# First projection of a decoder layer: two token parts in one 512-column matmul, and the bias rows copied from DRAM to DRAM

## The chip, the core and the metric

One core of a Trainium2 chip runs the whole layer in one launch. The metric is the device time of one execution in microseconds (us); lower is better. Engines are called as in the profile: PE (TensorE matmuls), PEld (its weight loads), DVE (VectorE), ACT (ScalarE), POOL (GpSimd, here an issuer of DMAs) and SP (SyncE, the issuer of the weight loads).

## The reference, cut to what matters

The layer takes x of 512 tokens by 2048 features, all in float32:

```
proj = x @ w_in                       # 2048 -> 12288 columns
u, gate_b, gate_c, q, k, v = split(proj)
y_conv = gate_b * causal_conv3(gate_c * u)
o_g    = dilated window attention of 3 groups x 8 heads, with a relative-position bias
x1 = layernorm(alpha * x + concat(y_conv, y_attn) @ w_out)
x2 = layernorm(alpha * x1 + conv_ffn(x1))      # w_up: 2048 -> 11264, w_down: 5632 -> 2048
```

The change touches `x @ w_in` and the table of bias rows (8 heads by 383 or 255 values for each of three groups) that the attention reads along its diagonals.

## The kernel before, in words

**The product.** Each float32 operand is split into a high part (rounded to the type that PE reads at full rate) and a low part (the remainder). A product a*b is taken as a_hi*b_hi + a_lo*b_hi + a_hi*b_lo. Weights go through `Op.front` (ACT writes `whi`, line 191) and `Op.back` (DVE writes `wlo`, line 194); for some operands DVE first forms a difference of two raw blocks (`tt`, line 181). The tokens are split once, at the start, into tiles X[name] = (high, low), each [128, 8, 256].

**Seven products in place of eight.** The first projection (w_in) and the up projection (w_up) are walked in pairs of 128-column blocks: 48 pairs for w_in, 44 for w_up. A pair is a 2x2 block product (two halves of the features, two halves of the tokens) done with seven products in the order `MAIN = [1, 5, 6, 3, 7, 4, 2]`. `product` (line 317) runs one: for each of 8 chunks of 128 features, three matmuls of 256 columns (lines 326 to 328): `whi` on the high tokens, `whi` on the low tokens, `wlo` on the high tokens, all summed into one half of a PSUM bank. A pair uses two banks, m (regions x1, x2) and n (x3, x4). After products 1, 5, 6 and 7 ACT copies the region to SBUF (`snap`, line 374). When a bank is complete, `combine` adds bank and copy on DVE: `bands` (line 572, one add of 512 columns per bank) for most pairs, `bands1` (line 581, two strided adds of 256 per bank) for the 24 of the 36 q, k and v pairs whose tokens are regrouped by stride 4.

**Order.** The program order of each engine is written by hand. `free` calls `pump`, which issues the next weight loads (three raw tiles of 1 MB, SP), and the `tt`, `whi` and `wlo` of operands up to four products ahead of PE; `later(n, fn)` and `tick` put a piece of work n products later, so a `combine` is issued behind the next product. Pair 0 is done plainly, pairs 1 to 5 have products 1 and 2 done early (before the other token tiles are ready), pairs 6 to 47 run all seven.

**Bias rows.** After the last of 12 convolution pairs `bias_setup` runs three times, some two pairs apart. It loads two small tables into one output tile (`otile1`, three slots shared with the pairs' outputs), a small matmul (line 560) and a DVE add (line 561) give 8 rows, and line 563, on POOL's queue, copies them to DRAM so that each of the 8 rows stands there 128 times (`seq_d[g]`: 8 heads x 128 copies x 384). The attention reads `seq_d` much later (lines 634 to 637). Pair outputs leave on the same POOL queue (`qkv_d`, line 611).

Of the kernel before, what the change touches and what calls it, by code (L numbers as in the profile page):

```python
# [12 lines left out]
F32 = mybir.dt.float32  # L13
# [67 lines left out]

class Chunks:
    def __init__(self, tiles, j):
        self.tiles, self.j = tiles, j

    def __getitem__(self, at):
        k = at[1]
        if isinstance(k, slice):  # L90
            return self.tiles[k.start // 2][:, self.j]
        return self.tiles[k // 2][:, self.j, k % 2]


@with_exitstack
def layer_kernel(ctx: ExitStack, tc: tile.TileContext, xT, x, w_in, w_out, w_up, w_down, cw, fw, lnp, lnc, table,
# [209 lines left out]

    pairb = {}

    def region(p, name):
        rg = pairb.setdefault(p, {})  # L310
        b = "m" if name in ("x1", "x2") else "n"
        if b not in rg:
            rg[b + "i"], rg[b] = get_bank()
        return rg[b][:, 256:] if name in ("x1", "x3") else rg[b][:, :256]


    def product(p, q, X, last):
        op = take()
        for q in q if isinstance(q, str) else [q]:
            xn, _, reg = PROD[q]  # L320
            xh, xl = X[xn]
            first = not _banks(q) & set(pairb.get(p, {}))
            ps = region(p, reg)
            for k in range(8):
                w = slice(k * P, (k + 1) * P)
                mm(ps, op.hi[:, w], xh[:, k], start=first and k == 0, stop=False, skip_group_check=True)  # L326
                mm(ps, op.hi[:, w], xl[:, k], start=False, stop=False, skip_group_check=True)  # L327
                mm(ps, op.lo[:, w], xh[:, k], start=False, stop=last and k == 7, skip_group_check=True)  # L328
        return op
# [33 lines left out]
                tick()  # L363
                hook()

    def run_pairs(pl, X, stile, otile, bands, done, hook=None):
        for p, seq, pre in pl:
            if pre or _plain(seq):
                continue
            sn = {b: stile(b).rearrange("p (a t) -> p a t", a=2) for b in "mn"}  # L370

            def snap(q):
                b, i = SNAP[q]
                nc.scalar.activation(sn[b][:, i], region(p, PROD[q][2]), AF.Copy)  # L374

            if 1 not in seq:
                snap(1)
            box = {"todo": 2}

            def combine(p, b, sn, box):  # L380
                if "o" not in box:
# [58 lines left out]
    def s_alloc(X, pools):  # L440
        for n in ("S2", "S4"):
            tiles = [None] * 4
            X[n] = (Chunks(tiles, 0), Chunks(tiles, 1))
        X["pools"] = pools

    def s_first(X, raw, k):
# [25 lines left out]
        low(X, "S4", ks, s4)  # L472

    def xtile(pool, n):
        return tuple(pool.tile([P, 8, 256], F32R, tag=n + s, name=nm(n + s)) for s in "hl")

# [53 lines left out]
        plan_work(XR[i], s_rest, X, raw, 2 * i)  # L530
    hook = schedule(todo)

    def keep1():
        return tp.tile([P, 2, 256], F32, tag="kp", name=nm("kp"), bufs=PRE1[0])
# [7 lines left out]
    def stile1(b):  # L542
        return tp.tile([P, 512], F32, tag="s" + b, name=nm("s" + b), bufs=2)

    def otile1():
        return tp.tile([P, 4, 256], F32, tag="o", name=nm("o"), bufs=3)
# [1 line left out]
    def bias_setup(g=0):  # L548
        if g == 0:
            held["tb"] = tp.tile([32, 3 * NH], F32, name="tb")  # L550
            nc.gpsimd.dma_start(held["tb"], table)
        a, b = [0, LA, LA + LB, LTOT][g:g + 2]
        v = otile1().rearrange("p a b -> p (a b)")
        oh, mk = v[:32, 0:b - a], v[:NH, 512:512 + b - a]
        nc.sync.dma_start(oh, onehot[:, a:b])
        nc.sync.dma_start(mk, mask[:, a:b])

        def finish():
            i, ps = get_bank()
# [54 lines left out]
    run_pairs(plan1, X, stile1, otile1, bands1, done1)  # L614
    ph1.close()


# [214 lines left out]

    a1s, chs, zas, zbs, exs = (ExitStack() for _ in range(5))
    a1p = mkpool(a1s, "a1p")
    A1h = a1p.tile([P, 2, 8, 256], F32R, tag="h", name="A1h")
    A1l = a1p.tile([P, 2, 8, 256], F32R, tag="l", name="A1l")
    chp = mkpool(chs, "chp")
    zbp = mkpool(zbs, "zbp")
    zap = mkpool(zas, "zap")
# [121 lines left out]
    s_alloc(X, {"S2": yap, "S4": xrp})  # L961
    s3p = mkpool(zas, "s3p")
    X["S3"] = xtile(s3p, "S3")
    X["A11"], X["A12"] = (A1h[:, 0], A1l[:, 0]), (A1h[:, 1], A1l[:, 1])

    todo = {}
    for i in range(4):
# [21 lines left out]
    def act_first(p, q):  # L989
        if p < FT - 1:  # L990
            return
        if q == 2:
            act_load(0, xrp, "S1h", nc.gpsimd)
            act_load(1, xrp, "S1l", nc.gpsimd)
            for s in "hl":
                act[s] = a1p.tile([P, 2, 4, S], F32R, tag=s, name=nm("A" + s))
        if q in (6, 3):
            n = (6, 3).index(q)
            act_split(n, act["h"][:, n], act["l"][:, n])
# [200 lines left out]
```

## Time and profile before

| | us |
|---|---|
| three runs | 2672.46, 2673.99, 2676.10 (median 2673.99) |
| profiled execution | 2674.91 |
| its span, first to last instruction | 2673.0 |
| PE busy | 2624.3 (98%) |
| DVE busy | 2015.5 (75%) |
| ACT busy | 1159.3 (43%) |

A sum of expected savings is made against the profiled execution, 2674.91 us, since the durations come from it. Busy is the time in which at least one instruction of the engine ran; the stages have different limits, so these shares are averages. The first projection takes about the first 1020 us, attention and the output projection follow up to about 1260, the up projection up to about 2120, and the down projection the rest.

### The profile page before, as it was taken

How to read it: one execution, taken by the hardware profiler on the slowest of the kernel's cores; microseconds unless marked ns; L12 is line 12 of the kernel's file. 1: busy time of each engine (PE TensorE's matmuls, PEld its weight loads, DVE VectorE, ACT ScalarE, POOL GpSimd, SP SyncE). 2: the span in 40 equal slices, each digit the busy share in tenths (PEclk: the TensorE clock that was granted, in tenths of full speed). 3: DMA queues.
4: the chain of work that ended last, by engine and by line, in shares of the span. 5: the costliest groups of instructions: out<-in, count | busy, mean ns of one | idle time of the engine just before them, and what ended most of it. 6: DMA issues, size and time to landing. Idle time of an engine off the chain costs nothing.

```text
span 2673.0 us, 45078 instructions
## 1 busy us (share of the span) xinstructions
PE 2624.3 (98%) x19114; PEld 2497.2 (93%) x19114; DVE 2015.5 (75%) x2293; ACT 1159.3 (43%) x1617; POOL 124.4 (5%) x214
## 2 busy tenths in 40 slices
PE   9999889999999999999999999999999999999998
PEld 8999789999999998888999999999999998888886
DVE  7987557777777777666899888888888875675557
ACT  5444334444444444434655555555555553222220
POOL 0000000000000002221000000000000000000000
PEclk9999989999999999999999999999999999999999
DMA  7433653333333338644543333333333354434331
GB/s 240 166 103 128 111 138 125 134 129 132 135 123 139 134 119 312 221 160 160 182 144 131 117 123 111 123 123 108 126 119 111 127 181 156 149 142 148 120 126 63
DMA packets 70905, 376.69 MB, mean 141 GB/s; under 512 B 10608, under 2 KB 14440, under 8 KB 36016
## 3 DMA queue, kind: packets, MB, share of 16 engines
q1 hardware_dynamic: 51680, 311.47, 34.0%
q0 software_dynamic: 19024, 62.34, 7.3%
q8 instruction: 150, 2.46, 0.4%
q14 instruction: 51, 0.42, 0.1%
HBM read 324.95 MB, written 48.81 MB: 140 GB/s over the span
## 4 chain that ended last, share of the span: by engine, by line
PE 88%; DVE 5%; DMA 4%; ACT 1%; issue 1%; SPq 0%; DVEq 0%; POOL 0%; ACTq 0%
PE bk L326 21%; PE bk L328 21%; PE bk L327 21%; PE bk L423 8%; PE bk L421 8%; PE bk L422 8%; DMA raw<-in_w_in_dram 2%; DMA seq_d<-o 2%; DVE wlo L194 1%; DVE tt L181 1%; PE bk L744 1%; PE bk L690 1%; PE bk L674 0%; ACT whi L191 0%; PE bk L736 0%
## 5 line engine op out<-in xcount | busy, mean ns | idle before, releaser
L191 ACT ACTIVATE whi<-raw 128x1024 fp32r<-128x1024 f32 x394 | 416.0, 1058 | 631.9 <-PE bk L423 219.0
L194 DVE TENSOR_TENSOR wlo<-raw,whi 128x1024 fp32r<-128x1024 f32 x394 | 480.7, 1223 | 216.0 <-ACT whi L191 215.9
L194 DVE TENSOR_TENSOR wlo<-tt,whi 128x1024 fp32r<-128x1024 f32 x360 | 440.5, 1224 | 210.1 <-ACT whi L191 209.5
L191 ACT ACTIVATE whi<-tt 128x1024 fp32r<-128x1024 f32 x360 | 379.6, 1054 | 220.1 <-PE bk L327 122.7
L326 PE MATMUL bk<-S,whi 128*128 128x256 f32 x1440 | 409.2, 284 | 12.4 <-ACT sm L374 11.5
L327 PE MATMUL bk<-S,whi 128*128 128x256 f32 x1440 | 408.4, 284 | 0.0
L328 PE MATMUL bk<-S,wlo 128*128 128x256 f32 x1440 | 408.4, 284 | 0.0
L326 PEld LDWEIGHTS bk<-S,whi 128*128 128x128 f32 x1440 | 277.5, 193 | 13.6 <-ACT sm L374 11.9
L327 PEld LDWEIGHTS bk<-S,whi 128*128 128x128 f32 x1440 | 277.5, 193 | 0.0
L328 PEld LDWEIGHTS bk<-S,wlo 128*128 128x128 f32 x1440 | 277.4, 193 | 0.0
L181 DVE TENSOR_TENSOR tt<-raw,tt 128x1024 f32<-128x1024 f32 x180 | 219.1, 1217 | 36.6 <-DMA raw<-in_w_in_dram 36.6
L326 PE MATMUL bk<-A22h,whi 128*128 128x256 f32 x752 | 212.8, 283 | 0.0
L327 PE MATMUL bk<-A22l,whi 128*128 128x256 f32 x752 | 212.8, 283 | 0.0
L328 PE MATMUL bk<-S3h,wlo 128*128 128x256 f32 x752 | 212.8, 283 | 0.0
L327 PE MATMUL bk<-S3l,whi 128*128 128x256 f32 x752 | 212.8, 283 | 0.0
L326 PE MATMUL bk<-S3h,whi 128*128 128x256 f32 x752 | 212.8, 283 | 0.0
L328 PE MATMUL bk<-A22h,wlo 128*128 128x256 f32 x752 | 212.8, 283 | 0.0
L328 PE MATMUL bk<-S1h,wlo 128*128 128x256 f32 x720 | 205.1, 285 | 6.2 <-DVE wlo L194 6.2
L326 PE MATMUL bk<-A1h,whi 128*128 128x256 f32 x720 | 205.2, 285 | 0.6 <-ACT S L932 0.6
L326 PE MATMUL bk<-S1h,whi 128*128 128x256 f32 x720 | 204.7, 284 | 0.0
L327 PE MATMUL bk<-S1l,whi 128*128 128x256 f32 x720 | 204.7, 284 | 0.0
L328 PE MATMUL bk<-A1h,wlo 128*128 128x256 f32 x720 | 204.4, 284 | 0.0
(225 smaller groups left out, 6435.4 us busy)
## 6 DMA issues: line engine op xcount, KB each, us to landing
raw<-in_w_in_dram SPq DMA_DIRECT2D x97, 1024.0 KB, 4.9
raw<-in_w_up_dram SPq DMA_DIRECT2D x89, 1024.0 KB, 5.3
raw<-in_w_down_dram SPq DMA_DIRECT2D x44, 1024.0 KB, 4.9
qkv_d<-o POOLq DMA_DIRECT2D x36, 512.0 KB, 4.3
raw<-in_w_out_dram SPq DMA_DIRECT2D x16, 1024.0 KB, 6.8
act_d<-z POOLq DMA_DIRECT2D x44, 256.0 KB, 5.2
qk<-qkv_d SPq DMA_DIRECT2D x7, 1536.0 KB, 10.3
ar<-act_d SPq DMA_DIRECT2D x9, 1024.0 KB, 7.0
```

The lines of the kernel that those rows point to most:

```text
L181: nc.vector.tensor_sub(self.src, v[0], prev)
L191: nc.scalar.activation(self.hi, self.src, AF.Copy)
L194: nc.vector.tensor_sub(self.lo, self.src, self.hi.bitcast(F32))
L326: mm(ps, op.hi[:, w], xh[:, k], start=first and k == 0, stop=False, skip_group_check=True)
L327: mm(ps, op.hi[:, w], xl[:, k], start=False, stop=False, skip_group_check=True)
L328: mm(ps, op.lo[:, w], xh[:, k], start=False, stop=last and k == 7, skip_group_check=True)
L421: mm(banks[n], yh[:, tt], op.hi[:, w], start=first and i == 0, stop=False)
L422: mm(banks[n], yh[:, tt], op.lo[:, w], start=False, stop=False)
L423: mm(banks[n], yl[:, tt], op.hi[:, w], start=False, stop=last and i == 1)
L690: mm(ps[:, o:o + P], qk[:, 2 + 2 * g, rs], qk[:, 3 + 2 * g, rs], start=True, stop=True)
L744: nc.tensor.transpose(ps[:, i * P:(i + 1) * P], src[:, n, s:s + P], ident)
```

## The change

In pairs 6 to 47 of the first projection the high and the low tokens lie in one tile, and one 512-column matmul streams both; its halves go to the two halves of a bank, and the third matmul (256 columns) adds to the second half. Each region takes a bank of its own, so a pair uses four. ACT copies whole banks after products 1, 5 and 6, and a copy of x1 just ahead of one of the sums; for each of four output blocks DVE adds a bank and a copy (512 columns), and then the two halves (256 columns each). Pairs 0 to 5 and the up projection keep three matmuls a chunk. The bias rows go to a small DRAM table first, and from there to their 128 copies by a DRAM-to-DRAM copy whose outer dimension is the 128 copies. Two tiles of the up projection are merged into one each; nothing else of it changes.

```diff
+    def product_wide(p, q, X, last):
+        op = take()
+        xn, _, reg = PROD[q]
+        first = reg not in pairb.get(p, {})
+        ps = wide_region(p, reg)
+        for k in range(8):
+            w = slice(k * P, (k + 1) * P)
+            mm(ps.rearrange("p (a t) -> p a t", a=2), op.hi[:, w], X[xn].both(k), start=first and k == 0, stop=False,
+               skip_group_check=True)
+            mm(ps[:, 256:], op.lo[:, w], X[xn][0][:, k], start=False, stop=last and k == 7, skip_group_check=True)
+        return op
...
+    WSUM = {(0, 0): ("x2", 1), (1, 1): ("x1", 5), (0, 1): ("x4", "x1"), (1, 0): ("x3", 6)}
+    def run_wide(p, seq, X, stile, otile, put_block, done, hook):
...
+        def combine(block):
...
+            reg, other = WSUM[block]
+            if other == "x1":
+                u = stile("u")
+                nc.scalar.activation(u, pairb[p][other], AF.Copy)
+            else:
+                u = sn[other]
+            nc.vector.tensor_add(u, pairb[p][reg], u)
+            put_block(p, box["o"], block, u)
...
+            op = product_wide(p, q, X, PROD[q][2] not in {PROD[j][2] for j in left})
+            if q in (1, 5, 6):
+                sn[q] = stile(str(q))
+                nc.scalar.activation(sn[q], pairb[p][PROD[q][2]], AF.Copy)
+            for block, need in WNEED.items():
+                if block not in sent and not need & left:
+                    sent.add(block)
+                    later(2, functools.partial(combine, block))
...
     def xtile(pool, n):
-        return tuple(pool.tile([P, 8, 256], F32R, tag=n + s, name=nm(n + s)) for s in "hl")
+        return Wide(pool.tile([P, 2, 8, 256], F32R, tag=n, name=nm(n)))
...
-            nc.gpsimd.dma_start(seq_d[g, :, :, :b - a], mk[:, None].to_broadcast([NH, P, b - a]))
+            nc.gpsimd.dma_start(seq1_d[g, :, :b - a], mk)
+            nc.gpsimd.dma_start(seq_d[g, :, :, :b - a].rearrange("h p n -> p h n"),
+                                seq1_d[g, None, :, :b - a].to_broadcast([P, NH, b - a]))
...
+    def block1(p, o, block, u):
+        f, h = block
+        if PAIRS[p][2] == 0:
+            nc.vector.tensor_add(o[:, 2 * f + h], u[:, :256], u[:, 256:])
+            return
+        ov = o.rearrange("p a t -> p (a t)").rearrange("p (f r m) -> p f r m", f=2, r=4)
+        ua, ub = (u[:, 256 * i:256 * i + 256].rearrange("p (m r) -> p r m", r=4) for i in range(2))
+        nc.vector.tensor_add(ov[:, f, :, 64 * h:64 * h + 64], ua, ub)
```

## Rows read from the trace of the kernel before

**Rows 1.** The page's busy times, and the granted clock of PE in 40 equal slices of the span.

```profile
PE 2624.3 (98%) x19114; PEld 2497.2 (93%) x19114; DVE 2015.5 (75%) x2293; ACT 1159.3 (43%) x1617; POOL 124.4 (5%) x214
PEclk9999989999999999999999999999999999999999
```

**Rows 2.** Busy time by stretch. Columns: the stretch, its length, then busy us (instructions) of PE, PEld, DVE, ACT and POOL, granted clock, DMA share, GB/s.

```profile
152.00:172.00 20.00, 20.00 (x169) 20.00 (x168) 14.08 (x14) 8.51 (x11) 0.00 (x0) 1.00 0.31 105
172.00:193.00 21.00, 21.00 (x177) 21.00 (x176) 18.72 (x19) 9.78 (x13) 0.00 (x0) 1.00 0.31 106
193.00:213.00 20.00, 20.00 (x169) 20.00 (x168) 15.27 (x15) 8.51 (x11) 0.53 (x1) 1.00 0.38 135
280.00:380.00 100.00, 76.30 (x568) 74.08 (x567) 46.37 (x46) 27.69 (x37) 4.42 (x6) 0.87 0.63 118
380.00:600.00 220.00, 220.00 (x1832) 220.00 (x1832) 163.77 (x161) 93.00 (x121) 7.87 (x11) 1.00 0.38 133
800.00:1005.00 205.00, 205.00 (x1711) 205.00 (x1710) 151.00 (x148) 86.41 (x112) 8.06 (x12) 1.00 0.37 130
1010.00:1020.00 10.00, 10.00 (x85) 10.00 (x84) 4.70 (x6) 4.01 (x6) 1.13 (x3) 1.00 1.00 410
1410.00:1900.00 490.00, 490.00 (x4085) 490.00 (x4085) 430.64 (x442) 257.12 (x341) 13.51 (x25) 1.00 0.36 117
```

**Rows 3.** Two matmuls of PE in order of time in the first projection (start, duration), 256 columns each; 25 matmuls stand between them.

```profile
499.79 0.28 PE L326 MATMUL bk<-S1h,whi 128*128 128x256 f32 x1
502.91 0.28 PE L328 MATMUL bk<-S,wlo 128*128 128x256 f32 x1
```

**Rows 4.** The same in the down projection, 512 columns each; 18 matmuls stand between them.

```profile
2499.67 0.39 PE L422 MATMUL bk<-wlo,Ah 128*128 128x512 f32 x1
2503.98 0.39 PE L423 MATMUL bk<-whi,Al 128*128 128x512 f32 x1
```

**Rows 5.** The chain of waits between 276 and 376 us (start, us, what), its DMA pieces.

```profile
278.90 40.53 DMA seq_d<-o
...
322.21 23.27 DMA raw<-in_w_in_dram
...
351.19 21.18 DMA raw<-in_w_in_dram
```

**Rows 6.** Who waited for whom between 276 and 382 us (us in total, times, longest), the rows that bear on the bias rows' copies.

```profile
DVE tt L181 <- DMA raw<-in_w_in_dram: 36.6, 3, 15.5
...
DVE o L572 <- DMA seq_d<-o: 11.7, 1, 11.7
...
PE bk L326 <- ACT sm L374: 10.6, 1, 10.6
...
PE bk L560 <- DMA o<-in_onehot_dram: 6.9, 1, 6.9
...
PE bk L328 <- DVE wlo L194: 6.2, 2, 4.9
```

**Rows 7.** The page's DMA issues (size of one, median us from issue to landing).

```profile
raw<-in_w_in_dram SPq DMA_DIRECT2D x97, 1024.0 KB, 4.9
seq_d<-o POOLq DMA_DIRECT2D x2, 1020.0 KB, 29.1
seq_d<-o POOLq DMA_DIRECT2D x1, 1532.0 KB, 40.5
tb<-in_table_dram POOLq DMA_DIRECT2D x1, 3.0 KB, 2.8
```

**Rows 8.** The same between 270 and 400 us.

```profile
raw<-in_w_in_dram SPq DMA_DIRECT2D x10, 1024.0 KB, 20.0
qkv_d<-o POOLq DMA_DIRECT2D x5, 512.0 KB, 22.0
```

**Rows 9.** Mean busy share of the 16 DMA engines, in tenths, in 40 slices of 348.5 to 377 us, while the third bias copy ran.

```profile
DMA  0036697999976596999645345544554454545300
```

**Rows 10.** SP's queue in order of time (start, us).

```profile
281.54 11.20 SPq L156 DMA_DIRECT2D raw<-in_w_in_dram  x2
320.97 0.33 SPq L555 DMA_DIRECT2D o<-in_onehot_dram  x1
```

**Rows 11.** Three instructions of DVE and PE in order of time around 300 us (in brackets the idle time before and its end).

```profile
293.68 1.22 DVE L194 TENSOR_TENSOR wlo<-raw,whi 128x1024 fp32r<-128x1024 f32 x1 [0.18 <-ACT whi L191]
303.98 1.23 DVE L181 TENSOR_TENSOR tt<-raw,tt 128x1024 f32<-128x1024 f32 x1 [9.07 <-DMA raw<-in_w_in_dram]
306.39 0.39 PE L328 MATMUL bk<-S1h,wlo 128*128 128x256 f32 x1 [1.31 <-DVE wlo L194]
```

**Rows 12.** Groups of instructions by line and shape over the whole run (busy us, mean ns of one, idle before).

```profile
L194 DVE TENSOR_TENSOR wlo<-tt,whi 128x1024 fp32r<-128x1024 f32 x360 | 440.5, 1224 | 210.1 <-ACT whi L191 209.5
L887 DVE TENSOR_TENSOR zz<-zz,bk 128x512 f32<-128x512 f32 x144 | 97.7, 687 | 32.9 <-PE bk L423 32.4
L374 ACT ACTIVATE sn<-bk 128x256 f32<-128x256 f32 x94 | 36.1, 384 | 151.7 <-PE bk L328 151.7
L581 DVE TENSOR_TENSOR o<-bk,sn 128x256 f32<-128x256 f32 x48 | 27.6, 617 | 0.0
L572 DVE TENSOR_TENSOR o<-bk,sm 128x512 f32<-128x512 f32 x23 | 15.7, 683 | 0.0
L765 ACT ACTIVATE sa<-bk 128x512 f32<-128x512 f32 x8 | 4.7, 586 | 1.9 <-PE bk L759 1.9
```

**Rows 13.** The tile `kp`: the one contiguous DVE add of 256 columns (count, ns min/median/max, first and last start).

```profile
L350 DVE TENSOR_TENSOR o<-bk,kp x2: 416/420/425, 72.2 to 72.5; 128x256 f32<-128x256 f32 x2
```

**Rows 14.** DVE and PE at the end of the first projection, in order of time.

```profile
1020.51 1.15 DVE L581 TENSOR_TENSOR o<-bk,sn 128x256 f32<-128x256 f32 x2
1022.10 2.36 DVE L287 TENSOR_TENSOR yc<-ycr,yc 128x1024 fp32r<-128x1024 f32 x2 [0.44 <-ACT yc L286]
1022.86 0.48 PE L421 MATMUL bk<-whi,yc 128*128 128x512 f32 x1
```

More of the change, by code (lines that the diff above doesn't have):

```diff
@@ L55 @@
 NWARM = 6
+SLOT, SBUFS = {"1": "m", "5": "n", "6": "6", "u": "u"}, {"6": 1, "u": 1}
 XS, XL, XF, XR = 4, (0, 0, 1, 4), (1, 2, 3, 6), (7, 9, 11, 12)
@@ L80, in _banks, with __init__, __getitem__, both @@
     return {"m" if PROD[i][2] in ("x1", "x2") else "n" for i in (q if isinstance(q, str) else [q])}
+class Wide:
+    def __init__(self, t):
+        self.t = t
+    def __getitem__(self, j):
+        return self.t[:, j]
+    def both(self, k):
+        return self.t[:, :, k]
 class Chunks:
@@ L92, in __getitem__, with __init__, both @@
         return self.tiles[k // 2][:, self.j, k % 2]
+class WideChunks:
+    def __init__(self, tiles):
+        self.tiles = tiles
+    def __getitem__(self, j):
+        return Chunks(self.tiles, j)
+    def both(self, k):
+        return self.tiles[k // 2][:, :, k % 2]
 @with_exitstack
@@ L130, in layer_kernel @@
     seq_d = dram.tile([3, NH, P, 384], F32, name="seq_d")
+    seq1_d = dram.tile([3, NH, 384], F32, name="seq1_d")
     stA_d = dram.tile([NH, S, 2], F32, name="stA_d")
@@ L307, in layer_kernel, with wide_region @@
     pairb = {}
+    def wide_region(p, name):
+        rg = pairb.setdefault(p, {})
+        if name not in rg:
+            rg[name + "i"], rg[name] = get_bank()
+        return rg[name]
+    def product_wide(p, q, X, last):
[9 more added lines that the diff above has]
+        return op
     def region(p, name):
@@ L320, in product @@
             xn, _, reg = PROD[q]
-            xh, xl = X[xn]
+            xh, xl = X[xn][0], X[xn][1]
             first = not _banks(q) & set(pairb.get(p, {}))
@@ L364, in run_plain, with run_pairs @@
                 hook()
-    def run_pairs(pl, X, stile, otile, bands, done, hook=None):
+    WSUM = {(0, 0): ("x2", 1), (1, 1): ("x1", 5), (0, 1): ("x4", "x1"), (1, 0): ("x3", 6)}
+    def run_wide(p, seq, X, stile, otile, put_block, done, hook):
+        sn, box = {}, {}
+        WNEED = {(0, 0): {1, 2}, (1, 1): {5, 6, 7}, (0, 1): {4, 6, 7}, (1, 0): {3, 6}}
+        def combine(block):
+            if "o" not in box:
+                box["o"], box["n"] = otile(), 4
+            reg, other = WSUM[block]
[6 more added lines that the diff above has]
+            put_block(p, box["o"], block, u)
+            box["n"] -= 1
+            for r in box.setdefault("free", {"x2": {(0, 0)}, "x1": {(1, 1), (0, 1)}, "x4": {(0, 1)}, "x3": {(1, 0)}}):
+                left = box["free"][r]
+                if block in left:
+                    left.discard(block)
+                    if not left:
+                        free_banks.append(pairb[p][r + "i"])
+            if box["n"] == 0:
+                del pairb[p]
+                done(p, box["o"])
+        sent = set()
+        for i, q in enumerate(seq):
+            left = set(seq[i + 1:])
+            op = product_wide(p, q, X, PROD[q][2] not in {PROD[j][2] for j in left})
[6 more added lines that the diff above has]
+                    later(2, functools.partial(combine, block))
+            free(op)
+            tick()
+            if hook:
+                hook(p, q)
+    def run_pairs(pl, X, stile, otile, bands, done, hook=None, put_block=None):
         for p, seq, pre in pl:
             if pre or _plain(seq):
+                continue
+            if 1 in seq and put_block:
+                run_wide(p, seq, X, stile, otile, put_block, done, hook)
                 continue
@@ L442, in s_alloc @@
             tiles = [None] * 4
-            X[n] = (Chunks(tiles, 0), Chunks(tiles, 1))
+            X[n] = WideChunks(tiles)
         X["pools"] = pools
@@ L531, in layer_kernel, with stile1 @@
     hook = schedule(todo)
+    def stile1(b):
+        return tp.tile([P, 512], F32, tag="s" + SLOT.get(b, b), name=nm("s" + b), bufs=SBUFS.get(SLOT.get(b, b), 2))
     def keep1():
-        return tp.tile([P, 2, 256], F32, tag="kp", name=nm("kp"), bufs=PRE1[0])
+        return stile1("u").rearrange("p (a t) -> p a t", a=2)
     run_pre(plan1, X, keep1, hook)
@@ L540, in layer_kernel @@
     nc.sync.dma_start(gb_t, lnc)
-    def stile1(b):
-        return tp.tile([P, 512], F32, tag="s" + b, name=nm("s" + b), bufs=2)
     def otile1():
@@ L613, in layer_kernel @@
     run_plain(plan1, X, otile1, done1, hook)
-    run_pairs(plan1, X, stile1, otile1, bands1, done1)
+    run_pairs(plan1, X, stile1, otile1, bands1, done1, None, block1)
     ph1.close()
@@ L834, in layer_kernel @@
     a1p = mkpool(a1s, "a1p")
-    A1h = a1p.tile([P, 2, 8, 256], F32R, tag="h", name="A1h")
-    A1l = a1p.tile([P, 2, 8, 256], F32R, tag="l", name="A1l")
+    A1 = a1p.tile([P, 2, 2, 8, 256], F32R, tag="A1", name="A1")
+    A1h, A1l = A1[:, 0], A1[:, 1]
     chp = mkpool(chs, "chp")
@@ L963, in layer_kernel @@
     X["S3"] = xtile(s3p, "S3")
-    X["A11"], X["A12"] = (A1h[:, 0], A1l[:, 0]), (A1h[:, 1], A1l[:, 1])
+    X["A11"], X["A12"] = Wide(A1[:, :, 0]), Wide(A1[:, :, 1])
     todo = {}
@@ L992, in act_first @@
         if q == 2:
[L993 to L996, printed above, removed]
+            t = xrp.tile([P, 2, 4, S], F32, tag="S1", name=nm("ar"))
+            for i in range(2):
+                act[i] = t[:, i]
+                nc.gpsimd.dma_start(act[i], act_d[:, 4 * i:4 * i + 4, :])
+            t = a1p.tile([P, 2, 2, 4, S], F32R, tag="A1", name=nm("A"))
+            act["h"], act["l"] = t[:, 0], t[:, 1]
         if q in (6, 3):
```

## The prediction

> **What bounds the kernel now.** I read the page first: PE is busy 98% of the span and its clock is at the upper level, 2.4 GHz, nearly everywhere [rows 1]. So time is gained by fewer PE nanoseconds or by filling PE's holes, and by nothing else. Next the busy times by stretch [rows 2]: between 380 and 600 us, and again from 800 to 1005, PE has no hole, and DVE is busy 163.8 of 220 us (74%). The one poor stretch is 280 to 380 us: PE is busy 76.3 us, its granted clock averages 0.87, and it starts 568 matmuls. At the undisturbed pace of 0.120 us (below) these are 68.2 us, so 31.8 us are lost there. Third, the chain of waits [rows 5] and the waits [rows 6] say why: one bias-row copy holds the chain for 40.5 us, then two raw weight loads for 23.3 and 21.2 us, where a raw load usually lands in 4.9 us [rows 7]; around the copies its median is 20.0 [rows 8]. Last, PE's pace from its own starts: 26 steps in 3.12 us give 120.0 ns for 256 columns [rows 3]; 19 steps in 4.31 us give 226.8 ns for 512 columns [rows 4].
>
> **The matmuls.** Before, a chunk is three steps of 256 columns: 360.0 ns. After, it is one of 512 and one of 256: 226.8 + 120.0 = 346.8 ns. The columns streamed are the same; what goes is one matmul with its weight load, and the two paces price it: 2 x 120.0 - 226.8 = 13.2 ns. Chunks: 42 pairs x 7 products x 8 = 2352. Saved: 2352 x 13.2 ns = 31.0 us, all of it on PE and so on the path. No row has a moving operand in two runs of 256 that lie apart, as the new one has. Bounds: 0 saved (each run costs what a matmul of 256 did) and 13.2 ns (as one run of 512). I take 13.2, by the only 512-column rows, whose instruction has the same shape.
>
> The trace thus charges about 13 ns for each matmul beside its columns: 120.0 and 226.8 ns are 13.3 and 13.5 ns above 256 and 512 columns at 2.4 GHz. The Trainium skill (TensorE: Matmul & The Clock Gate, section "Back-to-back issue gap") gives a gap of N / 2.4 GHz + 2.5 ns for a warm engine, which speaks against this change: by it a merged pair of matmuls saves 2.5 ns, and 2352 of them an estimated 5.9 us. This trace does not agree with the constant, so the sum keeps the rows' value.
>
> **The sums on DVE.** Before, a pair of the plain kind has 2 adds of 683 ns, 1.37 us; a strided pair has 4 of 617 ns, 2.47 us [rows 12]. After, every pair has 4 in-place adds of 512 columns from PSUM (687 ns, as L887 [rows 12]) and 4 adds of 256 in SBUF. The latter have no row; the contiguous add of 256 with a PSUM operand took 420 ns [rows 13] and the strided one 617 ns, which bound them. Plain pairs (18): 2.75 + 1.68 = 4.43 us, 3.06 more. Strided pairs (24): 2.75 + 1.68 to 2.47, at most 5.22, so 2.75 more; I take that end. Is there room? From 380 to 1005 us DVE used 163.8 / 220 x 20.16 = 15.0 us of a pair's 20.16 (7 x 24 x 0.120); after, about 17.8 of 19.42 (7 x 8 x 0.3468), 92%. The up projection runs at 430.6 / 490 = 88% without a PE hole [rows 2]. Cover: operands are made up to four products ahead, and when DVE stood idle 9.07 us for a raw load, PE lost 1.31 us [rows 11], so a DVE delay of some 7.8 us is hidden. One block needs ACT's copy of x1, which is queued behind a `whi` that waits for PE to finish the last product; DVE waits with it, and behind DVE stand the `tt` and `wlo` of the next pair. This costs about one product's time once a pair, inside the 7.8 us. The tight place is the convolution pairs: 14.08 + 18.72 + 15.27 = 48.1 us of DVE for three pairs [rows 2] become 57.2 of 58.3 us, 98%. I price this at 1.5 us in all, 0 at least; at most 0.5 us of PE wait in each of 42 pairs, 21 us.
>
> ACT's copies go from 4 x 0.384 to 4 x 0.586 us a pair [rows 12], 0.8 us more on an engine that is 42% busy: nothing, with the same 7.8 us as cover. Four banks a pair of eight are freed as the blocks are summed, so the next pair's first banks are free when it starts: nothing.
>
> **The bias rows.** Before, 8 rows x 128 copies are cut by an outer dimension of 8. While the third copy ran, the DMA share stayed at about half for a long stretch [rows 9]: half the engines worked, and a raw load, which needs all of them, waited for the busy half. After, the outer dimension is 128, like that of the loads that fill all 16 engines (share 1.00 from 1010 to 1020 us [rows 2]). At the same cost of a row and an engine the copies of 40.5 and 29.1 us [rows 7] take 20 and 15 us. The new first hop (12 KB) has its nearest row in a 3 KB transfer of 2.8 us [rows 7]; POOL's queue waits for it, with only `qkv_d` outputs behind it, which are not due for several microseconds: nothing on the path.
>
> What happens to the waits: the output slot held by the first copy (11.7 us on DVE, 10.6 on PE [rows 6]) is released after the first hop, so this wait goes. SP stood from 292.7 to 321.0 us for an output slot [rows 10], whose `qkv_d` transfer was queued behind the copy; with a copy of 20 us that wait shrinks to some 10 us, and the raw load behind it is late by as much. A raw load that lands during a copy may still take as long as the copy; the first such one was issued at 281.54 [rows 10], landed at 303.98 and cost PE 1.31 us [rows 11], so loads of up to about 20 us are hidden by the three raw tiles. What is late next is therefore that one held load: I leave 6 us of the 31.8 lost and gain 26. No row has a DRAM-to-DRAM copy: bounds are a gain of 32 (no stall left) and, if such a row moves so slowly that every load waits longer than now, a loss (a rival below).
>
> **The rest.** At the end of the projection the last block now has a copy (0.59 us) and two adds before the `yc` splits, and PE starts on `yc` 0.76 us after DVE's split begins [rows 14]: 1 us lost. The merged tiles of the up projection change no instruction: 0.
>
> **The sum**, against the profiled execution: 2674.9 - 31.0 - 26 + 1.5 + 1 = 2620.4; say 2620. That execution is 0.9 us above the median of the runs shown, which is below what counts here: a measurement can tell about 0.2%, 5 us.
>
> **The rivals.**
> 1. *The bias stall stays.* The DRAM source reads slowly, or the loads now meet the copy on all 16 engines instead of 8. For it: each copy moves as many rows as before, and raw loads already took as long as a copy did. Against it: the held slot goes in any case. If only that wait of 10.6 us is gained: 2674.9 - 31.0 - 10.6 + 2.5 = 2635.8. Chance 0.14.
> 2. *DVE becomes the bound.* For it: 92 to 98% busy, in order, with a wait on ACT in every pair. Against: 88% passes without a hole, and the cover is 7.8 us. At 0.5 us a pair: 2620.4 + 21 - 1.5 = 2640. Chance 0.07.
> 3. *The merged matmul saves little*, because the cost beside the columns goes with each run of 256 rather than with the instruction: 0 saved, 2674.9 - 26 + 2.5 = 2651. Against it speaks only that the 512-column rows have one run. The same section of the Trainium skill would also leave little, an estimated 2645. Chance 0.07.
> 4. *Slower than before.* One mechanism: the DRAM-to-DRAM copies crawl on all 16 engines, and no raw load lands before a copy ends. A load is hidden up to about 20 us, so three copies of T us stall PE for 3 x (T - 20). The rest of the change gains 28.5 us and the old stall of 31.8 goes, so it decides at 3 x (T - 20) = 60, T = 40 us for each copy; at T = 50 the time is 2674.9 - 60.3 + 90 = 2705. It needs a row to cost over three times what it does now per engine (29 to 40 us for 128 rows of an engine, now 64). Chance 0.05.
> 5. *No difference*: the savings of the matmuls are eaten by rivals 1 and 2 together, within 5 us of 2674. Chance 0.03.
>
> The forecast has the rest, 0.64, between 2612 (no stall left) and 2630.
>
> **How the numbers follow.** Faster by over 0.2%: the forecast and rivals 1 to 3, 0.92; the same 0.03; slower 0.05. The range from 2611 to 2640 takes in the forecast, rival 1 and half of rival 2: about 0.8.
>
> **What would show it.** PE starts in the first projection at 227 and 120 ns by turns, 0.347 us a chunk; weight loads fewer by 2352. DVE near 92% between pairs 12 and 47 with PE still without holes; PE waits on `wlo` in the convolution pairs would be rival 2. The two-hop copy should show DRAM share near full for 15 to 20 us a copy, raw loads below 20 us, no wait of DVE for `seq_d`, and PE above 92% from 270 to 370 us. Steps of 360 ns a chunk, or copies of over 40 us, would make the prediction wrong.

## The result and the profile after

| | before | after |
|---|---|---|
| median of the runs, us | 2674.87 (2672.46 to 2676.10, 4 runs) | 2634.77 (2634.13 to 2635.82, 4 runs) |
| profiled execution, us | 2674.91 | 2634.13 |
| its span, us | 2673.0 | 2632.4 |

The ratio is 0.9852 (0.9834 to 0.9869): 40.1 us faster, where 54 were forecast. The time lies inside the range, some 15 us above the number. Three measurements of the two traces place the gain. The first matmul of the head scores, right behind the projection, starts at 972.53 us where it started at 1019.63, 47.1 us earlier; the first transpose of the up projection starts at 1215.34 against 1255.95, 40.6 us earlier; and the spans differ by the same 40.6. So 47.1 us were won up to the end of the projection, and 6.5 of them were given back behind it, before the up projection starts.

The page's busy times, which answer to [rows 1]: 2352 matmuls fewer, which is the count of chunks, and 111.7 us more on DVE.

```profile
PE 2602.3 (99%) x16762; PEld 2365.4 (90%) x16762; DVE 2127.2 (81%) x2497; ACT 1201.5 (46%) x1617; POOL 125.8 (5%) x217
```

Busy time by stretch, columns as in [rows 2], with two short stretches at the end of the projection:

```profile
172.00:193.00 21.00, 20.28 (x116) 17.41 (x115) 18.64 (x23) 10.59 (x13) 0.00 (x0) 1.00 0.23 88
280.00:380.00 100.00, 100.00 (x565) 85.68 (x564) 87.17 (x97) 47.44 (x55) 6.69 (x10) 1.00 0.52 169
380.00:600.00 220.00, 220.00 (x1247) 190.70 (x1246) 193.83 (x212) 105.72 (x124) 7.88 (x11) 1.00 0.37 132
975.00:980.00 5.00, 1.46 (x10) 1.27 (x10) 1.02 (x2) 1.57 (x2) 0.72 (x1) 0.81 1.02 402
980.00:985.00 5.00, 4.96 (x12) 3.38 (x12) 5.00 (x8) 0.93 (x3) 0.00 (x0) 0.51 0.49 177
```

The poor stretch, 280 to 380 us, is full: PE is busy 100.00 us at clock 1.00, where it was 76.30 at 0.87. DVE is at 88% between 380 and 600 us, and PE has no hole there. The new holes are two small ones, that end at 187.60 and 246.99 us (0.72 and 0.87 us), and one of 3.5 us that ends at 979.54.

DMA issues between 270 and 400 us, which answer to [rows 7, 8] (size, median us to landing):

```profile
raw<-in_w_in_dram SPq DMA_DIRECT2D x13, 1024.0 KB, 4.9
seq_d<-seq_d POOLq DMA_DIRECT2D x2, 1020.0 KB, 8.7
seq_d<-seq_d POOLq DMA_DIRECT2D x1, 1532.0 KB, 9.2
seq_d<-o POOLq DMA_DIRECT2D x1, 12.0 KB, 1.7
```

The large copy took 40.5 us and now takes 9.2, the smaller ones 29.1 and now 8.7; the median of the raw loads is back at 4.9 us (20.0 before). That median is made by the loads between the copies: the three issued while a copy ran took 6.6 to 9.2 us, the first of them:

```profile
raw<-in_w_in_dram SPq DMA_DIRECT2D x1, 1024.0 KB, 9.2
```

The new first hop costs 1.6 to 1.7 us on POOL's queue.

Wide matmuls of PE in order of time (start, duration), which answer to [rows 3, 4]; between the first two rows stand 57 more of this width, between the last two 55:

```profile
214.75 0.39 PE L349 MATMUL bk<-A,whi 128*128 128x512 f32 x1
...
234.86 0.39 PE L349 MATMUL bk<-A,whi 128*128 128x512 f32 x1
...
489.88 0.40 PE L349 MATMUL bk<-S,whi 128*128 128x512 f32 x1
...
509.67 0.40 PE L349 MATMUL bk<-S,whi 128*128 128x512 f32 x1
```

The same stream has two paces. From 214.75 to 234.86 us 58 chunks pass in 20.11 us, 346.7 ns each: the forecast to the last digit. From 489.88 to 509.67 it is 56 chunks in 19.79 us, 353.4 ns. Followed in windows of 15 us, the projection runs at 353.3 ns up to a wait of PE at 187.60, at 346.7 from there to about 277 us, where the small matmuls of the first bias set-up stand, and at 353.3 from there to its end at 972.

DVE's groups of the sums between 380 and 600 us, which answer to [rows 12, 13]:

```profile
L427 DVE TENSOR_TENSOR s<-bk,s 128x512 f32<-128x512 f32 x33 | 22.5, 683 | 0.0
L687 DVE TENSOR_TENSOR o<-s 128x256 f32<-128x256 f32 x24 | 15.1, 628 | 0.8
...
L427 DVE TENSOR_TENSOR su<-bk,su 128x512 f32<-128x512 f32 x12 | 8.3, 692 | 21.9 <-ACT su L424 21.9
...
L683 DVE TENSOR_TENSOR o<-s 128x256 f32<-128x256 f32 x9 | 3.8, 426 | 0.3
```

The adds from PSUM take 683 to 692 ns (687 forecast); those in SBUF 426 ns contiguous and 628 strided, beside the rows of 420 and 617 that were taken. DVE waits 1.8 us a pair for ACT's copy of x1 (21.9 us before 12 adds), and PE has no hole in this stretch.

The instructions around the wait at 187.60, in order of time (start, us, in brackets the idle time before and its end):

```profile
179.34 0.58 ACT L424 ACTIVATE su<-bk 128x512 f32<-128x512 f32 x1
...
179.95 0.69 DVE L427 TENSOR_TENSOR su<-bk,su 128x512 f32<-128x512 f32 x1 [2.08 <-ACT su L424]
...
184.47 1.22 DVE L702 TENSOR_TENSOR o<-o,o 128x1024 f32<-128x1024 f32 x1
...
185.73 1.34 ACT L705 ACTIVATE o<-o,cw_t 128x512 f32<-128x512 f32 x2 [2.33 <-DVE o L702]
...
186.98 0.57 ACT L446 ACTIVATE s<-bk 128x512 f32<-128x512 f32 x1
...
187.60 0.50 PE L349 MATMUL bk<-S,whi 128*128 128x512 f32 x1 [0.72 <-ACT s L446]
```

This is a convolution pair. DVE waits 2.08 us for ACT's copy of x1 and works off the weight splits and sums queued behind it; then it forms a product of the convolution (line 702). ACT stands 2.33 us for that product with line 705, and behind 705 in ACT's queue is the copy of a bank (line 446) that PE needs. Such a wait of PE occurs twice, 1.6 us in all.

The end of the projection: who waited for whom between 940 and 1000 us (us in total, times, longest);

```profile
ACT yc L312 <- DMA ycr<-yc_d: 4.3, 1, 4.3
PE bk L514 <- ACT yc L312: 3.5, 1, 3.5
```

the load of `yc` that it waited for, in after and then in before (size, us to landing):

```profile
ycr<-yc_d POOLq DMA_DIRECT2D x1, 1024.0 KB, 14.3
```

```profile
ycr<-yc_d POOLq DMA_DIRECT2D x1, 1024.0 KB, 10.4
```

and the first and the 13th matmul on `yc`, in after, and the 13th in before (the first is in [rows 14], at 1022.86):

```profile
979.54 0.80 PE L514 MATMUL bk<-whi,yc 128*128 128x512 f32 x1 [3.54 <-ACT yc L312]
...
985.09 0.40 PE L514 MATMUL bk<-whi,yc 128*128 128x512 f32 x1
```

```profile
1025.78 0.39 PE L421 MATMUL bk<-whi,yc 128*128 128x512 f32 x1
```

The first load of `yc` is issued at 964.09 us, 8.4 us before the head scores start (9.0 in before), and lands 14.3 us later among other loads (the stretch from 975 to 980 shows DMA share 1.02), where it took 10.4. PE stands for 3.5 us, and between 980 and 985 us its granted clock is 0.51, the lower level of 1.2 GHz. In before PE did not wait for that load. From the first matmul of the head scores to the first on `yc` pass 7.0 us (3.2 in before), and from there to the 13th 5.55 us (2.92 in before). So 3.8 us were lost up to and in the wait and 2.6 behind it at the slower clock, which is 6.4 of the 6.5.

### The profile page after: what moved, and what is told of

Same layout as the page of the kernel before. It is cut to its first block, busy times and chain, and to the rows that moved or that the text cites. A ratio compares the mean times of both kernels' runs of the same rounds, so it can differ in the third digit from the quotient of the medians.

```text
span 2632.4 us, 40540 instructions
## 1 busy us (share of the span) xinstructions
PE 2602.3 (99%) x16762; PEld 2365.4 (90%) x16762; DVE 2127.2 (81%) x2497; ACT 1201.5 (46%) x1617; POOL 125.8 (5%) x217
## 4 chain that ended last, share of the span: by engine, by line
PE 90%; DVE 5%; ACT 2%; DMA 1%; issue 1%; SPq 0%; POOL 0%; DVEq 0%; ACTq 0%
PE bk L349 20%; PE bk L371 11%; PE bk L372 11%; PE bk L373 11%; PE bk L351 10%; PE bk L514 8%; PE bk L516 8%; PE bk L515 8%; DVE wlo L220 1%; DVE tt L207 1%; ACT whi L217 1%; PE bk L848 1%; DMA raw<-in_w_in_dram 1%; DMA ycr<-yc_d 1%; PE bk L794 0%
## 5 line engine op out<-in xcount | busy, mean ns | idle before, releaser
L349 PE MATMUL bk<-S,whi 128*128 128x512 f32 x1344 | 476.2, 398 | 1.6 <-ACT s L446 1.6
L371 PE MATMUL bk<-S,whi 128*128 128x256 f32 x1568 | 444.2, 283 | 1.8 <-ACT sm L467 0.9
L372 PE MATMUL bk<-S,whi 128*128 128x256 f32 x1568 | 443.7, 283 | 0.0
L373 PE MATMUL bk<-S,wlo 128*128 128x256 f32 x1568 | 443.7, 283 | 0.0
L351 PE MATMUL bk<-S,wlo 128*128 128x256 f32 x1344 | 377.3, 281 | 0.0
L349 PE MATMUL bk<-A,whi 128*128 128x512 f32 x1008 | 357.9, 398 | 0.0
L371 PE MATMUL bk<-A,whi 128*128 128x256 f32 x1248 | 355.6, 285 | 1.8 <-ACT whi L217 1.2
L373 PE MATMUL bk<-A,wlo 128*128 128x256 f32 x1248 | 354.9, 284 | 1.3 <-DVE wlo L220 1.1
L372 PE MATMUL bk<-A,whi 128*128 128x256 f32 x1248 | 354.7, 284 | 0.9 <-DVE A L313 0.9
L349 PEld LDWEIGHTS bk<-S,whi 128*128 128x128 f32 x1344 | 252.4, 188 | 64.4 <-ACT s L446 2.2
L371 PEld LDWEIGHTS bk<-S,whi 128*128 128x128 f32 x1568 | 301.0, 192 | 2.8 <-ACT z L467 1.7
L372 PEld LDWEIGHTS bk<-S,whi 128*128 128x128 f32 x1568 | 301.0, 192 | 0.0
L373 PEld LDWEIGHTS bk<-S,wlo 128*128 128x128 f32 x1568 | 301.0, 192 | 0.0
L351 PE MATMUL bk<-A,wlo 128*128 128x256 f32 x1008 | 283.0, 281 | 0.0
L351 PEld LDWEIGHTS bk<-S,wlo 128*128 128x128 f32 x1344 | 253.9, 189 | 0.0
L371 PEld LDWEIGHTS bk<-A,whi 128*128 128x128 f32 x1248 | 240.9, 193 | 2.7 <-ACT whi L217 1.6
L373 PEld LDWEIGHTS bk<-A,wlo 128*128 128x128 f32 x1248 | 240.9, 193 | 2.1 <-DVE wlo L220 2.1
L372 PEld LDWEIGHTS bk<-A,whi 128*128 128x128 f32 x1248 | 241.0, 193 | 1.4 <-DVE A L313 1.3
```

Of the source, the lines that this page charges most:

```text
L349: mm(ps.rearrange("p (a t) -> p a t", a=2), op.hi[:, w], X[xn].both(k), start=first and k == 0, stop=False, skip_group_check=True)
L351: mm(ps[:, 256:], op.lo[:, w], X[xn][0][:, k], start=False, stop=last and k == 7, skip_group_check=True)
```

## The experiments

Four questions were open: why a chunk takes 353.3 ns; which half of the new copy removed the stall; whether the 3.5 us at the end are the order of the loads or their bytes; and how much room DVE has left. Two readings of the 353.3 ns recur. A: what the prediction's rival 3 says, the second run of 256 columns costs. C: the stream has two paces, and a wait of PE can bring the other one.

**1. The bias rows alone**, before with the two-hop copy:

```diff
+    seq1_d = dram.tile([3, NH, 384], F32, name="seq1_d")
...
-            nc.gpsimd.dma_start(seq_d[g, :, :, :b - a], mk[:, None].to_broadcast([NH, P, b - a]))
+            nc.gpsimd.dma_start(seq1_d[g, :, :b - a], mk)
+            nc.gpsimd.dma_start(seq_d[g, :, :, :b - a].rearrange("h p n -> p h n"),
+                                seq1_d[g, None, :, :b - a].to_broadcast([P, NH, b - a]))
```

> The kernel before with only the two-hop copy of the bias rows. Theory (the copies' stall goes whole): the 31.8 us lost between 280 and 380 us come back, 2640 to 2645 us, raw loads near 6 us while a copy runs, no PE wait of over 1 us there. Rival (part of the loss of that stretch belongs to the pairs' outputs or to the order of the loads, not to the copies): 2650 to 2660 us.

Measured: 2643.49 us (2642.54 to 2643.90), 31.0 less than before on the same chip, ratio 0.988 (0.9864 to 0.9897). Busy time by stretch:

```profile
280.00:380.00 100.00, 100.00 (x828) 98.87 (x827) 72.23 (x71) 41.44 (x54) 7.42 (x11) 1.00 0.51 170
```

PE has no hole, so the whole stall of 31.8 us is gone, with the narrow matmuls as with the wide ones.

**2. The wide matmul alone**, after with the old copy (the diff of 1 the other way round):

> The changed kernel with the old one-hop copy of the bias rows. Theory (the parts add up, and a chunk takes 353.3 ns in place of 360.0): 2352 x 6.7 = 15.7 us gained, some 8 us given back in the convolution pairs and at the end of the projection, so 2665 to 2669 us. Rival (with DVE at 90% the old stall takes longer to recover from): the stretch of the copies loses over 40 us of PE time, 2672 us or more.

Measured: 2662.27 us (2658.45 to 2670.84), ratio 0.9956 (0.9941 to 0.9971). The stall is there again, now as a wait for `wlo` between 270 and 382 us; busy time by stretch and that wait:

```profile
280.00:380.00 100.00, 70.62 (x368) 59.78 (x368) 52.20 (x61) 29.70 (x36) 4.87 (x6) 0.84 0.56 116
```

```profile
PE bk L350 <- DVE wlo L219: 29.4, 3, 13.2
```

The gain of 12.2 us (median) is larger than expected, and the profiled execution shows something that was not in the expectation: behind the last hole, which ends at 378 us, the chunk takes 346.7 ns up to the end of the projection, in the same instructions that take 353.3 in after. Whether the two parts add up (31.0 + 12.2 = 43.2 against 40.1) can't be told, since the five runs here lie up to 12.4 us apart.

**3. High and low tokens of a chunk side by side**, so that the moving operand is one run of 512:

```diff
+class Near:
...
+    def both(self, k):
+        return self.t[:, k]
...
+    def xnear(pool, n):
+        return Near(pool.tile([P, 8, 2, 256], F32R, tag=n, name=nm(n)))
...
-    X = {n: xtile(xp, n) for n in ("A11", "A12", "S1")}
+    X = {n: xnear(xp, n) for n in ("A11", "A12", "S1")}
```

> The changed kernel with the high and low tokens of a chunk side by side, so that the 512-column matmul streams one run in place of two. Theory A (the second run costs 6.7 ns): a chunk takes 346.8 ns, 15 us less of PE in the first projection; at the end some of it may be lost to a later wait for yc, so 2620 to 2628 us. Theory B (the alternation of 512 and 256 columns costs it): 353.3 ns a chunk still, 2635 us.

Measured: 2635.72 us (2635.01 to 2636.15), ratio 0.9852 (0.9838 to 0.9867): no difference from after. Its wide matmuls, 57 chunks in 20.14 us, 353.3 ns:

```profile
489.76 0.40 PE L382 MATMUL bk<-S,whi 128*128 128x512 f32 x1
...
509.90 0.40 PE L382 MATMUL bk<-S,whi 128*128 128x512 f32 x1
```

It, too, has 346.7 ns between two waits of PE, at 187.67 and 247.06 us, and returns to 353.3 with the second. Reading A falls: with one run the same two paces appear.

**4. Fewer changes of width**: in each product first the eight wide matmuls, then the eight narrow ones:

```diff
         for k in range(8):
...
+            mm(ps.rearrange("p (a t) -> p a t", a=2), op.hi[:, k * P:(k + 1) * P], X[xn].both(k),
+               start=first and k == 0, stop=False, skip_group_check=True)
+        for k in range(8):
+            mm(ps[:, 256:], op.lo[:, k * P:(k + 1) * P], X[xn][0][:, k], start=False, stop=last and k == 7,
                skip_group_check=True)
-            mm(ps[:, 256:], op.lo[:, w], X[xn][0][:, k], start=False, stop=last and k == 7, skip_group_check=True)
```

> The changed kernel with eight 512-column matmuls of a product first and its eight 256-column matmuls behind them. Theory A (the second run costs 6.7 ns): 353 ns a chunk still, a 512-column step near 233 ns and a 256-column step at 120 ns, 2635 us. Theory B (alternation): steps of 226.8 and 120.0 ns, 346.8 ns a chunk, 2620 to 2628 us.

Measured: 2625.67 us (2624.12 to 2626.68), ratio 0.9814 (0.9800 to 0.9829), 9 us better than after. Six products in order of time:

```profile
491.69 2.00 PE L348 MATMUL bk<-A,whi 128*128 128x512 f32 x8
...
508.45 2.00 PE L348 MATMUL bk<-A,whi 128*128 128x512 f32 x8
```

(508.45 - 491.69) / 6 = 2.793 us a product, 349.2 ns a chunk. Against 8 x 346.7 = 2.774 a product still loses some 20 ns, with two changes of width in it.

**5. The second hop cut by 8 rows**, as the old copy was, but from DRAM:

```diff
-            nc.gpsimd.dma_start(seq_d[g, :, :, :b - a].rearrange("h p n -> p h n"),
-                                seq1_d[g, None, :, :b - a].to_broadcast([P, NH, b - a]))
+            nc.gpsimd.dma_start(seq_d[g, :, :, :b - a],
+                                seq1_d[g, :, None, :b - a].to_broadcast([NH, P, b - a]))
```

> The changed kernel with the second hop of the bias rows cut by its 8 rows, not by its 128 copies. Theory (the cut counts: half the engines, and raw loads wait for them): the DMA share stays near half for 15 us or more a copy, copies of 18 us or more in place of 9, raw loads of 12 to 20 us; PE holes of 0 to 15 us between 270 and 380 us, so 2635 to 2650 us. Rival (the source in DRAM and the freed output slot did it all): copies of about 9 us and no hole, 2635 us.

Measured: 2639.72 us (2639.46 to 2639.98, 2 runs), ratio 0.987 (0.985 to 0.989). Its DMA issues between 270 and 400 us, and the DMA share in 40 slices of 279 to 305 us, in it and in after:

```profile
raw<-in_w_in_dram SPq DMA_DIRECT2D x13, 1024.0 KB, 4.9
seq_d<-seq_d POOLq DMA_DIRECT2D x2, 1020.0 KB, 11.6
seq_d<-seq_d POOLq DMA_DIRECT2D x1, 1532.0 KB, 14.4
```

```profile
DMA  0000156555459999998639899853400000005654
```

```profile
DMA  0008999999999898979589951000000000898998
```

The cut does what the prediction read in [rows 9]: with 8 the share starts on a plateau of half, with 128 it is at nine tenths at once. But the copy takes 14.4 us against 9.2, a factor of 1.6, while it took 40.5 from SBUF with the same cut (35.3 in experiment 2): a factor of 2.5 to 2.8 came from the source. PE is busy 110.00 of 110 us from 270 to 380 here too, so a source in DRAM and a slot released early already remove the stall, and the cut adds nothing to that; raw loads issued beside these copies took 6.9 to 10.0 us. No run here separates the source from the slot. The 5 us by which this kernel is slower than after lie elsewhere: its chunk takes 353.3 ns all along, without the stretch at 346.7 (1.7 us), and behind the projection PE waits 6.8 us for `yc` and 1.4 for the first q and k, 8.2 against 3.5.

**6. The load of `yc` before the first q and k loads:**

```diff
-    a_load(0, nc.gpsimd)
-    ycr = [yc_load(0)]
+    ycr = [yc_load(0)]
+    a_load(0, nc.gpsimd)
```

> The changed kernel with the load of the convolution rows (ycr) issued ahead of the first head's q and k. Theory (the 3.5 us wait at the end of the projection, and the slow clock behind it, come from that load being last in a full stretch of DMA): the wait for yc goes, 6 us less, 2628 to 2630 us. Rival (the stretch is bound by its bytes): the wait moves to the first head's scores and the time stays within 2 us of 2635.

Measured: 2634.31 us (2632.63 to 2637.09), ratio 0.9853 (0.9837 to 0.9870), no difference. PE's waits between 940 and 1020 us:

```profile
PE bk L778 <- DMA qk<-qkv_d: 3.5, 1, 3.5
```

A wait of 3.5 us is there again, at the other load, and the granted clock falls behind this one too (0.67 between 975 and 980 us).

**7. The load of `yc` in two halves**, one before and one after q and k:

```diff
+            nc.gpsimd.dma_start(r[:, :2], yc_d[:, :2])
...
+    ycr = [yc_load(0)]
     a_load(0, nc.gpsimd)
-    ycr = [yc_load(0)]
+    nc.gpsimd.dma_start(ycr[0][:, 2:], yc_d[:, 2:4])
```

> The changed kernel with the convolution rows loaded in two halves, the first ahead of the first head's q and k and the second behind them, as PE needs them. Theory (PE waits at the end of the projection for bytes in the order of their issue, about 2.5 us for each MB): 0.5 MB less stands ahead of q and k than with the whole load first, so the wait there falls from 3.5 to about 2 us, and the wait for yc stays away: 2631 to 2633 us. Rival (the loads of weights on SP's queue fill the engines whatever POOL's order): 3 to 4 us of wait in another place, 2634 to 2636 us.

Measured: 2636.88 us (2635.36 to 2637.87), ratio 0.9862 (0.9847 to 0.9877).

```profile
PE bk L782 <- DMA qk<-qkv_d: 2.0, 1, 2.0
PE bk L514 <- ACT yc L312: 1.5, 1, 1.5
PE bk L516 <- DVE yc L313: 1.1, 2, 0.5
```

The waits on these loads add up to 4.6 us, more than in after, and nothing is gained. So neither of the two other orders helps. That the sum goes with the bytes isn't shown either: with the same loads in the order of after, PE's waits there add up to 1.5 us in experiment 10, 4.0 in 8, 4.4 in 4, 4.7 in 3, 5.8 in 9, 6.9 in 2 and 8.2 in 5, and `yc` takes 11.6 (experiment 10) to 19.2 us (experiment 5) to land. What sets this stays open. Which of the other loads to defer (the four raw blocks of `w_out`, 4 MB) wasn't tried.

**8. Two more adds of 512 columns a pair on DVE:**

```diff
             put_block(p, box["o"], block, u)
+            if box["n"] > 2:
+                nc.vector.tensor_add(u, u, u)
```

> The changed kernel with two more adds of 512 columns (0.69 us each) on DVE in each of the 42 pairs; their results are not used. Theory (DVE has cover until it is full): DVE at 95% from 380 to 950 us, no PE hole there, some 2 us more in the convolution pairs, 2635 to 2638 us. Rival (DVE is the bound already, through its wait for ACT's copy): each added microsecond shows, 42 x 1.4 = 58 us, 2690 us.

Measured: 2637.02 us (2636.72 to 2637.32, 2 runs), ratio 0.986 (0.984 to 0.9879).

```profile
380.00:600.00 220.00, 220.00 (x1247) 191.00 (x1246) 209.48 (x235) 105.31 (x122) 7.86 (x11) 1.00 0.36 132
```

At 95% on DVE PE still has no hole in the plain stretch. In the convolution pairs the wait grows from 1.6 us in two places to 2.6 in four.

**9. Waits put in by hand.** ACT's copy after product 5 is repeated six or seven times in the pairs 16, 21, 26, 31, 36 and 41, so that PE waits there:

```diff
-                nc.scalar.activation(sn[q], pairb[p][PROD[q][2]], AF.Copy)
+                for _ in range(6 + p % 2 if q == 5 and p in (16, 21, 26, 31, 36, 41) else 1):
+                    nc.scalar.activation(sn[q], pairb[p][PROD[q][2]], AF.Copy)
```

> The changed kernel with ACT's copy after product 5 done six or seven times in pairs 16, 21, 26, 31, 36 and 41, so that PE waits about a microsecond there (the copies repeat the same values). Theory C (a chunk of one wide and one narrow matmul has two paces, 346.7 and 353.3 ns, and a wait of PE draws the pace anew): after some of the six waits the pace is 346.7 until the next wait; the six waits cost 6 to 8 us, and each stretch of five pairs at the faster pace gives 1.9 us back, so 2630 to 2643 us. Rival D (the pace is set by the data, the layout or the load of the other engines): 353.3 ns in every stretch, 2641 to 2643 us.

Measured: 2638.87 us (2635.14 to 2641.64), ratio 0.9866 (0.9851 to 0.9880). Six waits between 340 and 860 us, 8.2 us in all. Around the fourth of them, PE in order of time:

```profile
623.65 0.39 PE L349 MATMUL bk<-S,whi 128*128 128x512 f32 x1
...
641.68 0.39 PE L349 MATMUL bk<-S,whi 128*128 128x512 f32 x1
...
644.58 0.50 PE L349 MATMUL bk<-S,whi 128*128 128x512 f32 x1 [1.69 <-ACT s L447]
...
645.03 0.40 PE L349 MATMUL bk<-S,whi 128*128 128x512 f32 x1
...
662.70 0.40 PE L349 MATMUL bk<-S,whi 128*128 128x512 f32 x1
```

Ahead of the wait 52 chunks take 18.03 us, 346.7 ns; behind it 50 take 17.67 us, 353.4. From the bias set-up on, by windows of 15 us:

| from, us | to, us | ns a chunk | waits of PE inside |
|---|---|---|---|
| 315 | 348.10 | 353.3 | |
| 348.10 | 644.58 | 346.7 | 447.14, 545.54 |
| 644.58 | 744.80 | 353.3 | |
| 744.80 | 972 | 346.7 | 843.83 |

Three of the six waits changed the pace, three did not, and between them it did not drift. The length of the wait doesn't decide: of the three of 1.69 to 1.70 us, the one at 644.58 changed the pace, those at 447.14 and 843.83 did not. This is reading C. The wider spread of the runs here and in experiment 2 (6.5 and 12.4 us against 1.7 of after) fits a pace that comes out differently from one execution to the next; that is argued, since only one execution of each was profiled.

**10. One change of width a product**: the groups of experiment 4, every second product with the narrow ones first:

```diff
+        flip[0] = not flip[0]
+        for n, wide in enumerate((flip[0], not flip[0])):
+            for k in range(8):
...
+                if wide:
+                    mm(ps.rearrange("p (a t) -> p a t", a=2), op.hi[:, w], X[xn].both(k), start=st_, stop=en,
+                       skip_group_check=True)
+                else:
+                    mm(ps[:, 256:], op.lo[:, w], X[xn][0][:, k], start=st_, stop=en, skip_group_check=True)
```

> As the kernel with eight wide and then eight narrow matmuls of a product, but every second product takes its narrow ones first, so that products meet wide to wide and narrow to narrow. Theory (each change between the two widths costs, some 10 ns as the grouped kernel's 20 ns a product with two changes): one change a product, 10 ns less for each of 294 products, 3 us: 2621 to 2624 us, 348 ns a chunk on average. Rival (what is left over 346.7 ns in the grouped kernel belongs to the two paces and not to the changes): 349 ns a chunk or 346.7 or 352, drawn by waits as before, 2618 to 2632 us.

Measured: 2618.03 us (2617.73 to 2618.83), ratio 0.9793 (0.9777 to 0.9809). It is the fastest of all, 55.9 us below before on the same chip. PE in order of time:

```profile
496.12 3.82 PE L355 MATMUL bk<-S,whi 128*128 128x512 f32 x16
499.77 2.08 PE L358 MATMUL bk<-S,wlo 128*128 128x256 f32 x16
501.69 3.82 PE L355 MATMUL bk<-S,whi 128*128 128x512 f32 x16
...
947.02 2.00 PE L355 MATMUL bk<-A,whi 128*128 128x512 f32 x8
```

From 496.12 to 947.02 us there are 81 such steps of two products: (947.02 - 496.12) / 81 = 5.567 us, 347.9 ns a chunk, so 2352 x (360.0 - 347.9) = 28.5 us of the 31.0 that the prediction counted. The time is lower than expected by some microseconds; PE's waits at the end of the projection were only 1.0 us for ACT's part of `yc` and 0.5 for DVE's, against 3.5 in after, and the granted clock stayed at 1.00 behind them (960 to 975 us).

## Why the prediction was right in kind and 15 us short

| term of the sum | forecast | measured | by |
|---|---|---|---|
| matmuls | -31.0 | -17.4 | the two paces |
| bias stall | -26 | -31.8, all of [rows 2]'s loss | 100.00 of 100 us busy; experiment 1 |
| convolution pairs | +1.5 | +1.6 | PE's two waits |
| end of the projection | +1 | +6.5 | 47.1 less 40.6 us |

Up to the end of the projection the first three terms give 31.8 + 17.4 - 1.6 = 47.6 us, where 47.1 were measured. With the last one, which is itself a difference of two measured gains, it is 41.1 against 40.6 between the spans.

That the time lies in the range is in part luck. The matmuls gave 13.6 us less than forecast and the end of the projection took 5.5 more, while the bias stall gave 5.8 more than counted. The 2634.8 measured is also nearly the 2635.8 of rival 1, whose mechanism, a stall that stays, did not occur.

**The matmuls** are the term that was mis-sized, and its reason was wrong too. The count of 2352 was right, and so was the pace of 346.8 ns, but only for one stretch: some 258 chunks, from 187.6 to 277 us, took 346.7 and saved 13.3 ns each (3.4 us), the other 2094 took 353.3 and saved 6.7 (14.0 us). The step added two paces that had each been read from an unmixed stream [rows 3, 4]; a stream that alternates between them was in no row, and the bounds were put on the number of runs in the operand instead. Experiment 3 shows that the runs don't matter. Experiments 9 and 10 show what does: the pace in an alternating stream is one of two, and with few changes of width it comes close to the sum of the unmixed ones. The Trainium skill (TensorE: Matmul & The Clock Gate, section "Back-to-back issue gap") would, by its gap of N / 2.4 GHz + 2.5 ns, have a merger save 2.5 ns, an estimated 5.9 us. Neither pace agrees, 6.7 and 13.3 ns being measured, and the measurement decides. The section calls this gap that of an isolated matmul, and here a weight load goes with each, so the prediction drew on it for a stream that it doesn't describe.

**The bias rows** were better than forecast, by the 6 us that the prediction had left lost. Its reason was a copy of 20 us that would hold one raw load. The factor of two for the cut was too high (1.6, from 14.4 to 9.2 us, in experiment 5); the source was not in the argument, and it made the larger factor (40.5 to 14.4 us). The Trainium skill (SBUF — State Buffer, section "Door 1: The DMA port swizzle (why `[64,N]` ≈ `[32,N]`)") says that the rate of a DMA on SBUF goes with how many of its ports the partitions reach, which eight neighbouring rows do with few. The two copies with the same cut and the same bytes agree with it in direction; no run here varied the rows, so the port itself isn't shown.

**DVE** was costed right: 88% from 380 to 600 us where 92% was forecast, no hole there, and the waits in the convolution pairs of the size and at the place that the prediction named as tight. The chain to them begins as it said, with DVE's wait for the copy of x1 and the `wlo` queued behind; it missed the last link, line 705, with which ACT in its turn waits for DVE. So PE waits there for a bank's copy and not, as was expected, for `wlo`. Rival 2 falls with experiment 8.

**The end of the projection** was costed by DVE's work alone, 1 us. What was late there was a load that the sum had at nothing: `yc` took 14.3 us to land where it had taken 10.4. Up to and in the wait 3.8 us were lost, and 2.6 at the clock of 0.51 behind it, read from the first and the 13th matmul on `yc`. Why the load took longer isn't shown. Experiments 6 and 7 gained nothing by another order. An earlier end of the projection alone doesn't explain it: experiment 1 gets there 31 us earlier than before and waits 0.4 us, and experiment 10, the fastest, waits 1.5.

The other rivals: rival 1 (the stall stays) and rival 4 (copies that crawl) fall with copies of 8.7 to 9.2 us, raw loads of 6.6 to 9.2 beside them and no hole. Rival 3 counted nothing saved, where 17.4 of 31.0 us were, and its mechanism falls with experiment 3.

**What stays open**: what decides which of the two paces follows a wait; whether the 6.7 ns, which are 16 cycles of 2.4 GHz, have to do with weight loads; why a change of width in the grouped kernels costs some 10 ns (20 ns a product with two, 20 ns for two products with one each) while an alternating stream at 346.7 ns pays nothing for it; and why the same loads behind the projection land faster in some kernels than in others.

## What to carry to other kernels

A pace read from an unmixed stream of matmuls is not yet the pace of a mixed one: where two widths alternate, bound the chunk from both sides, and group equal widths where the order is free. When a small table has to be replicated in DRAM, put it there once and copy from DRAM to DRAM; eight SBUF rows as a source cost more than the cut did. Price the first loads of the next stage along with the stage that is shortened, and a clock that can fall behind their wait: here the same loads in the same order cost PE waits of 1.5 to 8.2 us, and the clock another 2.6 in after.

## What was not expected of the hardware

- The same instructions in the same order ran at 346.7 or 353.3 ns for 512 + 256 columns, steady for hundreds of microseconds. The pace changed at some of PE's waits of 0.7 to 1.7 us and not at others of the same length, and in after also where the small matmuls of the bias set-up stood between.
- A copy of 1.5 MB from DRAM to DRAM took 9.2 us, and a raw load issued beside it also 9.2; from eight rows of SBUF it took 40.5, and the raw loads beside it 20.2 and 22.3.
- A wait of 3.5 us at the end of a projection that had run at clock 1.00 was followed by 5 us at clock 0.51, while behind waits of 1.0 and 0.5 us at the same place (experiment 10) it stayed at 1.00.
